# One more stick head, and the last sparse head, turned by DMA planes instead of TensorE; a gate block's halves moved up

## The chip, the cores and the metric

One core of one Trainium2 chip. The metric is device microseconds of the program, a median of three runs. In the profile the engines are PE (TensorE), ACT (ScalarE), DVE (VectorE), POOL (GpSimd) and SP (SyncE, which here only issues DMAs).

## What is computed

One block of a streaming encoder, for 512 frames of 1024 channels in f32. An input projection feeds two mixers of eight heads each:

```python
# A, sparse: the best n_sel keys of each query by an indexer's score, then softmax
logits = einsum(q, kg) * HEAD_DIM ** -0.5 + rel_bias[t5_bucket(sel - t)]
y_a = softmax(where(valid, logits, -inf)) @ vg
# B, stick-breaking: strictly causal, no softmax
log_keep = where(causal, log_sigmoid(-z), 0.0)
later = cumsum(log_keep, reverse=True) - log_keep
y_s = where(causal, exp(log_sigmoid(z) + later), 0.0) @ v
# merge, norm, gated MLP with a causal convolution of width 3, norm
merged = sigmoid(g_a + b0) * (y_a @ w_branch_dsa) + sigmoid(g_b + b1) * (y_s @ w_branch_sb)
x = layer_norm(ALPHA * x + merged @ w_out)
x = layer_norm(ALPHA * x + (gelu(causal_dwconv(x @ w_u)) * (x @ w_g)) @ w_ffn_out)
```

## The kernel before

Every f32 product goes over PE as three products of halves: a weight tile is split into a high half `whi`, rounded to PE's fast f32 format, and a rest `wlo`, and PE multiplies high by high, high by low and low by high. `Stream` (L52) loads the weight pieces in one fixed order, three ahead, into `raw`; its `_advance` (L88) has ACT write the high half (L104) and then either DVE or POOL subtract it (L113), or, for the keys in DMA_LO, ACT write minus the high half (L107) and a POOL DMA add the weights to it on landing (L110). gb0 to gb7, qa0 and ka0 go by DMA; ks1 and the four pieces of va have POOL's subtraction; qa1, ka1 and later have DVE's. `asp` says how many pieces ahead of their use are split.

The projections (`proj_t`, L227; 24 products of 128x512 each, one PSUM bank) are fillers: the list FILL orders them, and `fill` hands some of their products to PE between the steps of the heads. Stick heads 0 to 7 come first, then sparse heads a0 to a7. `tile` names in the profile drop numbers: `gb_ps` are the gate blocks of mixer B, `qa_ps` and `ka_ps` the queries and keys of the sparse heads, `va_ps` their values, which take four banks at once (`va_ps0` to `va_ps3`, the third and fourth being those that qa1 and ka1 had, free when DVE has made `qa1b` and `ka1b`). The program fixes each engine's order when it is built; `tc.issue_after(x)` keeps an instruction behind x in that order. Each engine then works strictly in its order, and an instruction that waits holds up all behind it.

A stick head h has its products z (`sb_head`, L523) turned by ACT into `keep` and `beta` (six sigmoids), scans of `keep` on DVE (`sb_sticks`, L541), and `beta` multiplied by them on POOL (L550). A sparse head has logits `l_ps` with bias and row minimum `mn` on DVE (L579), exponents on ACT (L582), and a division on DVE (L589). The weights must then be turned, so that keys lie on partitions. That goes in one of two ways:

- `turn_weights` (L439): ten transposes of 128x128 on PE into `tr_ps` (L450), three ACT copies `pth` (L453), three DVE rests `ptl` (L454). Stick heads 0 to 3 (`TURN = 4`) and a7.
- `send_planes` (L464): the f32 numbers as two planes of 16 bits. ACT copies the high ones (L469, into `keep` of the head, or `bm`), POOL or DVE the low ones (L470), and SP issues two DMA transposes into `pl` (L472). `join_planes` (L477): ACT and POOL or DVE put them together in `back` (L481, L482), ACT makes `pth` (L484), DVE `ptl` (L488). Stick heads 4 to 7, a0 to a6.

`weigh` (L498) multiplies them with the values on PE (`av_ps`, L504), eight products for a head that PE turned, ten for one that came by planes; `avt` and `yst` add the two halves up, and for every second head `ys1h`, `ys1l` split the pair.

At the first head by planes (i == TURN) ties hold the order: gb6's halves stand on ACT behind that head's `pth` (`st.behind`), ka0's copies and gb4's sigmoids behind gb6's halves. `beta`, `keep`, `bm`, `lg` and `pl`, `back`, `pth`, `ptl` have one or two buffers each, so that a head's planes wait until the head before has been read.

## Time and profile before

| | |
|---|---|
| runs (three) | median 748.91 us, 748.35 to 749.09 |
| profiled execution | 748.38 us, span 746.3 us, mean granted PE clock 0.997 |
| PE busy | 99% of the span |
| DVE, ACT, POOL busy | 76%, 54%, 20% |

A row of a timeline has the start, how long it took, engine, line, operation, out<-in by the program's names, shape, and in brackets the idle time before it and what ended that. Products on PE overlap: a row of 0.39 us is followed 0.23 us later by the next. A row of the chain has start, length and what ran.

### The profile page before, as it was taken

The numbers are of one execution on the slowest core, as the hardware profiler recorded it, in microseconds if no ns is written. First come the engines' busy times: TensorE is split into PE (matmuls) and PEld (weight loads), VectorE is DVE, ScalarE is ACT, GpSimd is POOL, SyncE is SP. The second block draws the span as 40 slices with busy tenths as digits, with TensorE's granted clock in tenths as the row PEclk, the third lists the DMA queues.
The fourth block names the chain that finished last, engine by engine and source line by source line (L and its number), as shares of the span: only waits on it lengthen the run. The fifth ranks groups of instructions, "written<-read, shape, count | busy, mean of one in ns | idle before, by whom it ended". The sixth has DMA issues, their size and how long they took to land.

```text
span 746.3 us, 9766 instructions
## 1 busy us (share of the span) xinstructions
PE 736.9 (99%) x3485; PEld 618.2 (83%) x3485; DVE 570.8 (76%) x907; ACT 406.7 (54%) x572; POOL 147.9 (20%) x161
## 2 busy tenths in 40 slices
PE   9999999999999999999999999999999999999995
PEld 7888888888888888888889888888888888888885
DVE  5569888999679898568755867676667677668995
ACT  6465867797785688645564533443444344345430
POOL 0002224365743331000101111011101101110011
PEclk9999999999999999999999999999999999999998
DMA  8445887896566554228732544444443444448532
GB/s 265 157 131 188 197 179 175 161 214 163 115 176 163 134 141 121 86 86 269 266 57 86 171 139 142 146 136 141 139 169 115 141 156 147 143 141 282 188 129 84
DMA packets 71007, 116.38 MB, mean 156 GB/s; under 512 B 39912, under 2 KB 40168, under 8 KB 70960
## 3 DMA queue, kind: packets, MB, share of 16 engines
q1 hardware_dynamic: 63680, 93.33, 41.5%
q0 software_dynamic: 5744, 18.38, 9.9%
q10 hardware_dynamic: 1536, 4.06, 2.1%
q8 instruction: 27, 0.44, 0.3%
q14 instruction: 20, 0.16, 0.1%
HBM read 95.93 MB, written 9.98 MB: 142 GB/s over the span
## 4 chain that ended last, share of the span: by engine, by line
PE 89%; DVE 4%; issue 2%; ACT 2%; POOL 2%; DMA 1%; DVEq 0%; POOLq 0%; ACTq 0%
PE u_ps L927 5%; PE u_ps L925 5%; PE g_ps L927 5%; PE g_ps L925 5%; PE u_ps L926 5%; PE g_ps L926 5%; PE m L1006 2%; PE m L1007 2%; PE m L1005 2%; PE av_ps L504 2%; PE ga_ps L235 2%; PE ga_ps L234 2%; PE gb_ps L235 2%; PE gb_ps L234 2%; PE ga_ps L233 2%
## 5 line engine op out<-in xcount | busy, mean ns | idle before, releaser
L104 ACT ACTIVATE whi<-raw 128x1024 fp32r<-128x1024 f32 (+1 forms) x124 | 124.0, 1002 | 150.3 <-PE g_ps L926 46.0
L113 DVE TENSOR_TENSOR wlo<-raw,whi 128x1024 fp32r<-128x1024 f32 (+1 forms) x105 | 123.9, 1181 | 38.7 <-ACT whi L104 38.0
L927 PE MATMUL u_ps<-x1h,wlo 128*128 128x512 f32 (+1 forms) x192 | 71.4, 372 | 0.0
L925 PE MATMUL u_ps<-x1h,whi 128*128 128x512 f32 (+1 forms) x192 | 71.3, 372 | 0.0
L926 PE MATMUL u_ps<-x1l,whi 128*128 128x512 f32 (+1 forms) x192 | 71.3, 371 | 0.0
L925 PE MATMUL g_ps<-x1h,whi 128*128 128x512 f32 (+1 forms) x184 | 69.9, 380 | 0.0
L926 PE MATMUL g_ps<-x1l,whi 128*128 128x512 f32 (+1 forms) x184 | 69.9, 380 | 0.0
L927 PE MATMUL g_ps<-x1h,wlo 128*128 128x512 f32 (+1 forms) x184 | 69.9, 380 | 0.0
L926 PEld LDWEIGHTS u_ps<-x1l,whi 128*128 128x128 f32 x192 | 36.2, 188 | 6.3
L927 PEld LDWEIGHTS u_ps<-x1h,wlo 128*128 128x128 f32 x192 | 36.2, 188 | 6.3
L925 PEld LDWEIGHTS u_ps<-x1h,whi 128*128 128x128 f32 x192 | 36.2, 188 | 6.2
L927 PEld LDWEIGHTS g_ps<-x1h,wlo 128*128 128x128 f32 x184 | 34.6, 188 | 6.6
L926 PEld LDWEIGHTS g_ps<-x1l,whi 128*128 128x128 f32 x184 | 34.6, 188 | 6.6
L925 PEld LDWEIGHTS g_ps<-x1h,whi 128*128 128x128 f32 x184 | 34.6, 188 | 6.5
L948 DVE TENSOR_TENSOR t<-raw 128x512 f32<-128x512 f32 x11 | 7.6, 692 | 38.7 <-DMA raw<-in_w_fo_dram 38.4
L562 POOL TENSOR_TENSOR bm<-win,score 128x256 f32<-128x256 f32 (+2 forms) x24 | 26.2, 1119 | 33.9 <-DMA pl<-bm 29.1
L981 DVE TENSOR_TENSOR hF<-g_ps,c 128x512 f32<-128x512 f32 x22 | 15.1, 687 | 20.9 <-PE g_ps L927 20.9
L967 POOL MEMSET u<- 128x2 f32 x22 | 2.1, 98 | 146.0 <-ACT whi L104 101.0
L973 ACT ACTIVATE c<-c,cwt 128x512 f32<-128x512 f32 x22 | 15.9, 725 | 25.2 <-DVE c L972 24.9
L823 POOL TENSOR_TENSOR rstd<-rstd,mhalf 128x1 f32<-128x1 f32 x8 | 7.7, 959 | 104.5 <-DVE rstd L822 104.5
L423 DVE MAX8 m<-score 128x8 f32<-128x256 f32 (+2 forms) x48 | 26.6, 556 | 0.9
L550 POOL TENSOR_TENSOR beta<-beta,keep 128x1280 f32<-128x1280 f32 x8 | 21.7, 2709 | 26.9 <-DVE keep L547 20.9
(578 smaller groups left out, 2086.7 us busy)
## 6 DMA issues: line engine op xcount, KB each, us to landing
raw<-in_w_fi_dram SPq DMA_DIRECT2D x44, 512.0 KB, 3.3
raw<-in_w_t_dram SPq DMA_DIRECT2D x32, 512.0 KB, 3.4
raw<-in_w_fo_dram SPq DMA_DIRECT2D x26, 512.0 KB, 4.1
wlo<-in_w_t_dram POOLq DMA_DIRECT2D x14, 512.0 KB, 5.9
raw<-in_w_br_dram SPq DMA_DIRECT2D x8, 512.0 KB, 3.7
raw<-in_w_o_dram SPq DMA_DIRECT2D x8, 512.0 KB, 4.0
raw<-in_w_v_dram SPq DMA_DIRECT2D x7, 512.0 KB, 4.5
raw_b<-in_w_fo_dram SPq DMA_DIRECT2D x6, 512.0 KB, 5.2
```

Of the source, the lines that this page charges most:

```text
L104: self.high = nc.scalar.activation(hi[:, :w], t[:, :w], AF.Copy).ins
L113: self.done[key] = eng.tensor_sub(lo[:, :w], t[:, :w], r32(hi[:, :w])).ins
L234: nc.tensor.matmul(ps[:M], wh[:, c], xl[k], start=False, stop=False)
L235: nc.tensor.matmul(ps[:M], wl[:, c], xh[k], start=False, stop=(k == KC - 1))
L423: nc.vector.max(m8, sc)
L550: nc.gpsimd.tensor_mul(beta, beta, keep[:, 1:ATT + 1])
L562: nc.gpsimd.tensor_add(bm[:, OFF[j]:OFF[j] + N], win[:, 512 - N:512], score[j])
L925: nc.tensor.matmul(ps[:, c], wh[:, kc], x1h[:, k, c], start=(k == 0), stop=False)
L926: nc.tensor.matmul(ps[:, c], wh[:, kc], x1l[:, k, c], start=False, stop=False)
L927: nc.tensor.matmul(ps[:, c], wl[:, kc], x1h[:, k, c], start=False, stop=(k == KC - 1))
L973: nc.scalar.activation(c, c, AF.Gelu_apprx_tanh, bias=cwt[:, f, 3:4])
L981: nc.vector.tensor_mul(F[:, o:o + 2].rearrange("p a b -> p (a b)"), gps_, c)
```

## The change

Stick head 3 no longer goes over PE (TURN 4 to 3), nor does a7. TIED = 4 keeps the ties of the first head by planes at head 4, and adds some. Head 3's planes are joined ahead of head 4's being sent; gb6's halves stand behind head 6's sigmoids and ahead of head 5's plane copy and head 4's `pth` (which is now made inside ka0, `finish_join`); gb4's and gb5's sigmoids stand behind the halves of gb6 and gb7; a7's planes get a buffer of their own among the `keep` tiles, and its `pth` stands behind the half that follows ga3's copies. The core of the diff:

```diff
-TURN = 4
+TURN = 3
+TIED = 4
...
-                if key == "gb6":
+                if key in ("gb6", "gb7"):
                     self.behind = self.high
...
+    def finish_join():
+        with tc.issue_after(st.highs["gb6"]):
+            parts = waiting.pop()()
+        waiting.append(parts)
+        with tc.issue_after(firsts[1]):
+            select_some(ROUNDS[TIED] - 2)
...
-    def send_planes(lg, bm, eng=nc.vector):
+    def send_planes(lg, bm, eng=nc.vector, last=False):
...
+        if last:
+            pl = padded(bp, [128, ATT + 1], tag="keep", bufs=2, name="pl")[:, 0:ATT].bitcast(U16)
+            pl = pl.rearrange("p (a b c) -> p a b c", a=2, c=128)
...
-        eng.tensor_copy(halves16(back)[:, 0], got[:, 0])
+        copied.append(eng.tensor_copy(halves16(back)[:, 0], got[:, 0]).ins)
+        if first:
+            waiting.append(lambda: halves_of(back))
+            return waiting
+        return halves_of(back)
+
+    def halves_of(back):
         th, tl = turned()
         high = nc.scalar.activation(th, back, AF.Copy).ins
...
-            return (send_planes(lg, bm) if h < H - 1 else lg), last.ins
+            return send_planes(lg, bm, last=h == H - 1), last.ins
...
+            if t == "ka0":
+                st.asp = 2
             ps = yield from proj_t(t)
...
+                if t == "ka0":
+                    st.asp = 3
+                    finish_join()
+                    st.behind = firsts[0]
+                with tc.issue_after(firsts[0]) if t == "ka0" else nullcontext():
                     qk[t] = stack_hl(ps, "k", 4, t)
...
-                with tc.issue_after(st.highs["gb6"]) if n == 4 else nullcontext():
+                with tc.issue_after(st.highs[f"gb{n+2}"]) if n in (4, 5) else nullcontext():
...
-        last = sb_sticks(*following, behind={TURN + 1: "gb5", TURN + 2: "gb6"}.get(i))
+        last = sb_sticks(*following, {TIED + 1: "gb5", TIED + 2: "gb6"}.get(i))
         if i < TURN:
             return following[0], last
+        if i == TIED + 1:
+            return following, last
...
+        if i == TIED + 1:
+            st.asp, st.behind = 3, ups[h + 1]
+            st._advance(st.used)
+            with tc.issue_after(st.highs["gb6"]):
+                weights = send_planes(*weights[0], nc.gpsimd), weights[1]
...
-        turns = w == "s" and i < TURN or not following
+        if not following:
+            fill_until("ga3")
+            with tc.issue_after(ups["ga3"]):
+                parts = join_planes(weights[0])
+            st.behind = tops[-1]
+        turns = w == "s" and i < TURN
...
+            ahead = not turns and i < TIED
+            if ahead:
+                last = sb_scans(*following)
+                with ExitStack() as ties:
+                    for ins in (last, ups[h + 1], st.high, st.added):
+                        ties.enter_context(tc.issue_after(ins))
+                    parts = join_planes(weights[0], nc.gpsimd)
+                beta, keep = following
+                with tc.issue_after(copied[-1]):
+                    nc.gpsimd.tensor_mul(beta, beta, keep[:, 1:ATT + 1])
+                with tc.issue_after(highs_of[-1]):
+                    following = send_planes(beta, keep, nc.gpsimd), last
+                joins[h + 2] = highs_of[-1]
```

The change also moves what stands on the engines. On ACT before, around the halves of gate block 6 (`whi_30`, `wlo_30`; `keep_1525` is head 5's plane copy, `pth_1582` head 4's high part, `whi_31` belongs to gb7):

```order
L348 DMA qa0b_1617<-qa0b_1617 64x1024
L469 ACTIVATE keep_1525<-beta_1524 128x1280
L484 ACTIVATE pth_1582<-back_1579 128x1280
L104 ACTIVATE whi_30_1624<-raw_30_1622 128x1024
L107 ACTIVATE wlo_30_1625<-whi_30_1624 128x1024
L338 ACTIVATE ka0a_1676<-ka0_ps_1629 64x512
L339 ACTIVATE ka0b_1677<-ka0_ps_1629 64x512
L104 ACTIVATE whi_31_1684<-raw_31_1682 128x1024
L631 ACTIVATE gb4_1755<-gb4_ps_1689,bgt_105 128x512
L107 ACTIVATE wlo_31_1685<-whi_31_1684 128x1024
```

and now (`keep_1500` is head 5's copy, `pth_1659` head 4's high part, `back_1711` joins head 5's high plane, `whi_32` is qa1's high half):

```order
L349 DMA qa0b_1595<-qa0b_1595 64x1024
L105 ACTIVATE whi_30_1637<-raw_30_1600 128x1024
L108 ACTIVATE wlo_30_1638<-whi_30_1637 128x1024
L487 ACTIVATE keep_1500<-beta_1499 128x1280
L663 ACTIVATE gb4_1748<-gb4_ps_1682,bgt_105 128x512
L508 ACTIVATE pth_1659<-back_1567 128x1280
L339 ACTIVATE ka0a_1669<-ka0_ps_1602 64x512
L340 ACTIVATE ka0b_1670<-ka0_ps_1602 64x512
L105 ACTIVATE whi_31_1677<-raw_31_1675 128x1024
L108 ACTIVATE wlo_31_1678<-whi_31_1677 128x1024
L499 ACTIVATE back_1711<-pl_1642 128x1280
L105 ACTIVATE whi_32_1752<-raw_32_1750 128x1024
```

gb6's halves went from behind head 5's copy and head 4's `pth` to ahead of both; gb4's sigmoids too come ahead of `pth`, and qa1's high half follows `back` directly, without head 7's sigmoids between.

On PE before, where gate block 7 ends and qa1 begins (`whi_32`, `wlo_32` are qa1's halves):

```order
L233 MATMUL gb7_ps_1896<-xh7_346,whi_31_1684 128x512
L234 MATMUL gb7_ps_1896<-xl7_347,whi_31_1684 128x512
L235 MATMUL gb7_ps_1896<-xh7_346,wlo_31_1685 128x512
L233 MATMUL qa1_ps_1930<-xh0_131,whi_32_1759 128x512
L504 MATMUL av_ps_1808<-pth_1721,vs0_704 128x384
L234 MATMUL qa1_ps_1930<-xl0_132,whi_32_1759 128x512
L235 MATMUL qa1_ps_1930<-xh0_131,wlo_32_1760 128x512
L573 MATMUL l_ps_1945<-ka0a_1676,qa0a_1616 128x512 x2
```

and now, where gb7 begins:

```order
L525 MATMUL av_ps_1687<-ptl_1660,vs3_713 128x128
L234 MATMUL gb7_ps_1889<-xh0_131,whi_31_1677 128x512
L235 MATMUL gb7_ps_1889<-xl0_132,whi_31_1677 128x512
L234 MATMUL qa1_ps_1923<-xh0_131,whi_32_1752 128x512
L235 MATMUL qa1_ps_1923<-xl0_132,whi_32_1752 128x512
L236 MATMUL qa1_ps_1923<-xh0_131,wlo_32_1753 128x512
L234 MATMUL qa1_ps_1923<-xh1_185,whi_32_1752 128x512
L235 MATMUL qa1_ps_1923<-xl1_186,whi_32_1752 128x512
```

qa1 went from behind all of gb6 and gb7 to behind the first two products of each; 22 of its 24 products stand there, and the rest of gb6 and gb7 follows them.

On PE before, where va takes its fourth bank (`whi_34`, `whi_35` are halves of va's first two pieces, `l_ps_2081` the last logits of a1):

```order
L270 MATMUL va_ps0_2092<-whi_35_1926,xh2_227 128x512
L270 MATMUL va_ps1_2093<-whi_35_1926,xh2_227 128x512
L270 MATMUL va_ps2_2094<-whi_35_1926,xh2_227 128x512
L270 MATMUL va_ps3_2095<-whi_34_1892,xh0_131 128x512
L271 MATMUL va_ps3_2095<-wlo_34_1893,xh0_131 128x512
L272 MATMUL va_ps3_2095<-whi_34_1892,xl0_132 128x512
L270 MATMUL va_ps3_2095<-whi_34_1892,xh1_185 128x512
L271 MATMUL va_ps3_2095<-wlo_34_1893,xh1_185 128x512
L272 MATMUL va_ps3_2095<-whi_34_1892,xl1_186 128x512
L270 MATMUL va_ps3_2095<-whi_35_1926,xh2_227 128x512
L573 MATMUL l_ps_2081<-ka0b_1677,qa0b_1617 128x256 x2
L271 MATMUL va_ps0_2092<-wlo_35_1927,xh2_227 128x512
```

and now (`va_ps3_2088` is the fourth bank, `l_ps_2074` the last logits of a1):

```order
L525 MATMUL av_ps_1973<-ptl_1833,vs3_713 128x128
L271 MATMUL va_ps2_2087<-whi_34_1885,xh0_131 128x512
L271 MATMUL va_ps3_2088<-whi_34_1885,xh0_131 128x512
L599 MATMUL l_ps_2074<-ka0b_1670,qa0b_1595 128x256 x2
L272 MATMUL va_ps0_2085<-wlo_34_1886,xh0_131 128x512
L273 MATMUL va_ps0_2085<-whi_34_1885,xl0_132 128x512
L272 MATMUL va_ps1_2086<-wlo_34_1886,xh0_131 128x512
L273 MATMUL va_ps1_2086<-whi_34_1885,xl0_132 128x512
```

Of va's products, 21 stood ahead of the fourth bank's first one and 28 ahead of a1's last logits; now three and four do, and the others follow.

More of the change, by code (lines that the diff above doesn't have):

```diff
@@ L432, in select_some @@
             pass
+    firsts, copied, highs_of, joins = [], [], [], {}
+    waiting = []
+    def finish_join():
[4 more added lines that the diff above has]
+            select_some(ROUNDS[TIED] - 2)
+    sent, tops = [], []
     def turned():
@@ L462, in halves16 @@
         return t.bitcast(U16).rearrange("p (c two) -> p two c", two=2)
-    def send_planes(lg, bm, eng=nc.vector):
+    def send_planes(lg, bm, eng=nc.vector, last=False):
         src = halves16(lg)
         own = bm[:, 0:ATT].bitcast(U16).rearrange("p (a c) -> p a c", a=2)
-        pl = bp.tile([128, 2, ATT // 128, 128], U16, tag="pl", bufs=1, name="pl")
-        nc.scalar.activation(own[:, 1], src[:, 1], AF.Copy)
+        if last:
+            pl = padded(bp, [128, ATT + 1], tag="keep", bufs=2, name="pl")[:, 0:ATT].bitcast(U16)
+            pl = pl.rearrange("p (a b c) -> p a b c", a=2, c=128)
+        else:
+            pl = bp.tile([128, 2, ATT // 128, 128], U16, tag="pl", bufs=1, name="pl")
+        sent.append(nc.scalar.activation(own[:, 1], src[:, 1], AF.Copy).ins)
+        highs_of.append(sent[-1])
         eng.tensor_copy(own[:, 0], src[:, 0])
@@ L473, in send_planes @@
         return pl
-    firsts = []
     def join_planes(pl, eng=nc.vector, first=False):
@@ L481, in join_planes @@
         nc.scalar.activation(halves16(back)[:, 1], got[:, 1], AF.Copy)
-        eng.tensor_copy(halves16(back)[:, 0], got[:, 0])
+        copied.append(eng.tensor_copy(halves16(back)[:, 0], got[:, 0]).ins)
[4 more added lines that the diff above has]
+    def halves_of(back):
         th, tl = turned()
         high = nc.scalar.activation(th, back, AF.Copy).ins
-        if first:
-            st.behind = high
-            firsts.append(high)
-        low = nc.vector.tensor_sub(tl, back, r32(th)).ins
-        if first:
-            firsts.append(low)
+        tops.append(high)
+        highs_of.append(high)
+        firsts[:] = high, nc.vector.tensor_sub(tl, back, r32(th)).ins
         h, l = (t.rearrange("p (s c) -> p s c", c=128) for t in (th, tl))
@@ L536, in sb_head, with sb_scans @@
             c = slice(OFF[grp[0]], OFF[grp[0]] + o)
-            nc.scalar.activation(keep[:, c], ps[:, :o], AF.Sigmoid, scale=-0.125)
+            with tc.issue_after(joins[h]) if h in joins else nullcontext():
+                nc.scalar.activation(keep[:, c], ps[:, :o], AF.Sigmoid, scale=-0.125)
             ups[h] = nc.scalar.activation(beta[:, c], ps[:, :o], AF.Sigmoid, scale=0.125).ins
         return beta, keep
-    def sb_sticks(beta, keep, behind=None):
+    def sb_scans(beta, keep):
         for j in (1, 0, 2, 3):
@@ L548, in sb_sticks @@
                                                 op1=ALU.max)
+        return scan.ins
+    def sb_sticks(beta, keep, behind=None):
+        last = sb_scans(beta, keep)
         with tc.issue_after(st.done[behind]) if behind else nullcontext():
             nc.gpsimd.tensor_mul(beta, beta, keep[:, 1:ATT + 1])
-        return scan.ins
+        return last
     def dsa_head(q, k, h):
@@ L625, in filler @@
             elif kind in ("ks", "ka"):
-                with tc.issue_after(st.highs["gb6"]) if t == "ka0" and firsts else nullcontext():
+                if t == "ka0":
[3 more added lines that the diff above has]
+                with tc.issue_after(firsts[0]) if t == "ka0" else nullcontext():
                     qk[t] = stack_hl(ps, "k", 4, t)
@@ L701, in values_of @@
         fill_until(f"v{w}")
-        ends = weigh(parts, vals[w], h, pair[w])
+        ends = weigh(parts.pop() if parts is waiting else parts, vals[w], h, pair[w])
         if h % 2 == 1:
@@ L725, in tile_block @@
             ends = values_of(*joined)
-        turns = w == "s" and i < TURN or not following
+        if not following:
[4 more added lines that the diff above has]
+        turns = w == "s" and i < TURN
         if turns:
-            if not following:
-                fill(GAP)
             parts, lows = turn_weights(weights[0])
         if w == "s" and i + 1 < H:
-            with tc.issue_after(lows) if turns else nullcontext():
-                following = advance(i + 1)
+            ahead = not turns and i < TIED
[11 more added lines that the diff above has]
+                joins[h + 2] = highs_of[-1]
+            else:
+                with tc.issue_after(lows) if turns else nullcontext():
+                    following = advance(i + 1)
             with tc.issue_after(following[1]):
-                if not turns:
+                if not turns and not ahead:
                     with tc.issue_after(ups[h + 1]), tc.issue_after(st.high):
-                        parts = join_planes(weights[0], nc.gpsimd, i == TURN)
-                if i == TURN:
+                        parts = join_planes(weights[0], nc.gpsimd, i == TIED)
+                if i == TIED:
                     select_some(2)
-                    with tc.issue_after(firsts[1]):
-                        select_some(ROUNDS[i] - 2)
                 else:
@@ L751, in tile_block @@
                     with ExitStack() as ties:
-                        for ins in (emptied["va"] if (w, h) == ("a", 1) else ()) + (following[1], ups[(h + 1) % H]):
+                        late = (emptied["va"] if (w, h) == ("a", 1) else ()) + ((sent[-1],) if i + 2 == len(heads) else ())
+                        for ins in late + (following[1], ups[(h + 1) % H]):
                             ties.enter_context(tc.issue_after(ins))
```

4 lines of the change are left out of this document (2 added, 2 removed).

## The prediction

> **What bounds the kernel now.** I read the page first, then the waits of the tensor engine (PE), then the chain of waits in the stretch that the change rewrites, then timelines of single engines. The page gives busy time, and the chain that ended last by engine:
>
> ```profile
> PE 736.9 (99%) x3485; PEld 618.2 (83%) x3485; DVE 570.8 (76%) x907; ACT 406.7 (54%) x572; POOL 147.9 (20%) x161
> ```
>
> ```profile
> PE 89%; DVE 4%; issue 2%; ACT 2%; POOL 2%; DMA 1%; DVEq 0%; POOLq 0%; ACTq 0%
> ```
>
> All that PE waited for, in the view of waits (us in total, times, longest):
>
> ```profile
> PE idle_ps L210 <- DVE idle L207: 1.2, 1, 1.2
> PE bs_ps L603 <- DVE ka2b L341: 0.4, 1, 0.4
> PE bs_ps L605 <- DVE wlo L113: 0.2, 1, 0.2
> ```
>
> PE is the bound: work taken from it is time, unless a new wait gives it back. But in one stretch the others are nearly as late as PE. The chain of waits leaves PE with the first two of these rows and comes back with the last two:
>
> ```profile
> 189.74 1.25 POOL ys2l L517
> 190.99 3.61 POOL wlo L113
> ```
>
> ```profile
> 253.70 0.70 DVE ka2b L341
> 254.54 0.47 PE bs_ps L603
> ```
>
> Between 190 and 254 us a chain over GpSimd (POOL), ScalarE (ACT), VectorE (DVE) and transposes runs as long as PE's own work there; PE has under a microsecond to spare. Whoever moves that chain against PE's order pays, and the change moves both.
>
> **The change part by part.** *PE's pace.* The 24 products of ka1 begin between the first two of these rows of PE (the third is used further down):
>
> ```profile
> 186.68 0.39 PE L233 MATMUL ka_ps<-xh,whi 128*128 128x512 f32 x1
> ```
>
> ```profile
> 192.12 0.39 PE L270 MATMUL va_ps<-whi,xh 128*128 128x512 f32 x1
> ```
>
> ```profile
> 200.94 0.41 PE L573 MATMUL l_ps<-ka0b,qa0b 128*128 128x256 f32 x2
> ```
>
> (192.12 − 186.68) / 24 = 0.227 us for 512 columns.
>
> *Transposes off PE, head 3 and a7.* A head's ten transposes in the tile's view, and PE's rows around head 3:
>
> ```profile
> L450 PE MATMUL tr_ps<-ident,lg x10: 272/272/273, 308.5 to 309.5; 128*128 128x128 f32 x10
> ```
>
> ```profile
> 133.60 1.25 PE L450 MATMUL tr_ps<-ident,beta 128*128 128x128 f32 x10
> 134.61 0.47 PE L234 MATMUL gb_ps<-xl,whi 128*128 128x512 f32 x1
> ```
>
> By starts they take 134.61 − 133.60 = 1.01 us, and the product behind them lasts 0.08 longer than the usual 0.39: 1.1 us a head. Against that, weights times values goes as ten products in place of eight, over the same 2 x 1280 columns, 1.14 us at the pace. A head with ten took, in the chain,
>
> ```profile
> 256.75 1.33 PE av_ps L504 x10
> ```
>
> so the two extra cost between 0 and 0.2 us; I take 0.1, since eight already pay part of the surplus. Net −1.0 us for head 3 and −1.0 for a7, on the binding engine.
>
> A rule of the Trainium skill speaks against this: VectorE: DVE Perf Modes, section The three transpose paths, gives 390 ns for a 128x128 transpose on TensorE and 1309 ns by DMA, and the page's rules for kernel authors prefer TensorE where the result may land in PSUM. By its figures ten would be 3.9 us of PE and each head would save 2.8 us more, and the slower DMA would matter only where PE waits for it. The row differs: the ten follow each other at 0.10 us. The sum goes by the row.
>
> *Cover of the two new round trips.* PE's gb3 ended, and the copy behind which head 3's high part now stands began, at
>
> ```profile
> 139.27 0.39 PE L233 MATMUL qa_ps<-xh,whi 128*128 128x512 f32 x1
> ```
>
> ```profile
> 140.78 1.05 ACT L107 ACTIVATE wlo<-whi 128x1024 fp32r<-128x1024 f32 x1
> ```
>
> so the part is there at 140.78 + 1.05 + 1.26 = 143.1, while PE does 36 products of qa0 and ka0 first: 139.27 + 36 x 0.227 = 147.4. Four microseconds of cover; if the transposes took that much longer, their excess would be paid. For a7 the high part stands on ACT behind a half that waits for gate block ga4; between that and a7's products PE does ga5, 24 x 0.227 = 5.4 us, against 1.04 + 1.26 + 1.5 for half, high and low part. Both cost 0; 0.7 is the most that I would give a7, were its transposes late.
>
> *The first products of qa1.* PE's new order puts 22 products of qa1 ahead of most of gate block 6. They need both halves of raw_32. ACT makes the high one behind head 5's `back` copy, which waits for head 5's planes, whose copy now stands behind gb6's halves. ACT's rows, before:
>
> ```profile
> 150.76 1.68 ACT L481 ACTIVATE back<-pl 128x1280 uint16<-128x1280 uint16 x1 [0.99 <-DMA pl<-keep]
> ```
>
> ```profile
> 156.20 1.27 ACT L469 ACTIVATE keep<-beta 128x1280 uint16<-128x1280 uint16 x1 [0.18 <-POOL keep L470]
> 157.38 1.26 ACT L484 ACTIVATE pth<-back 128x1280 fp32r<-128x1280 f32 x1
> 158.54 1.04 ACT L104 ACTIVATE whi<-raw 128x1024 fp32r<-128x1024 f32 x1
> ```
>
> ```profile
> 164.41 1.65 ACT L481 ACTIVATE back<-pl 128x1280 uint16<-128x1280 uint16 x1
> ```
>
> From `back` to the copy of head 5 (`keep`) took 156.20 − 150.76 = 5.4 us. Now avt and ys1h of the second pair (estimated 1.2 together) and gb6's two halves (2.1) stand in between: the copy begins at 150.76 + 5.4 + 3.3 = 159.5 and ends at 160.7. From pth to the next `back` took 164.41 − 157.38 = 7.0, now without gb6's halves 4.9: ACT is free at 165.6. The transposes of the copy land 4.9 behind it, also at 165.6 (issues by queue, 120 to 200 us):
>
> ```profile
> pl<-keep SPq DMA_TRANSPOSE x8, 4.9
> ```
>
> `back` (1.6 with its overlap), the high half (1.04) and DVE's low half,
>
> ```profile
> 173.88 1.21 DVE L113 TENSOR_TENSOR wlo<-raw,whi 128x1024 fp32r<-128x1024 f32 x1
> ```
>
> end at 169.5. PE comes to its first product with that low half at 168.0, from gb5's last three products, which began at
>
> ```profile
> 166.93 0.40 PE L233 MATMUL gb_ps<-xh,whi 128*128 128x512 f32 x1
> ```
>
> 166.93 − 1.0 + (3 + 6) x 0.227: the six are two each of gb6, gb7 and qa1. So PE would wait 1.5 us. But head 4's planes, which set 150.76, went with both transposes back to back; a load now parts them, and the first may land a microsecond sooner, which leaves 0.5. I take the middle, s = 1.0, with the ends 0 and 3 (every landing a microsecond later).
>
> *The wait for ka1's bank.* PE's new order has, behind qa1 and ka1, one product for each of va's four banks and then the last logits of sparse head a1; before, 28 products of va stood ahead of the logits. The fourth bank is ka1's, free when DVE has made ka1b, and the logits wait for the row minimum right behind ka1b on DVE. Without a wait PE would come to the logits 24 products earlier than 200.94: 200.94 − 1.0 − 24 x 0.227 + s = 194.5 + s. When is the minimum there? ACT and DVE before:
>
> ```profile
> 183.13 1.28 ACT L582 ACT_TABLE_LOAD   x1
> ```
>
> ```profile
> 184.94 0.59 ACT L509 ACTIVATE avt<-av_ps 64x512 f32<-64x512 f32 x1
> ```
>
> ```profile
> 186.48 0.63 ACT L516 ACTIVATE ys2h<-yst 128x512 fp32r<-128x512 f32 x1 [0.95 <-DVE yst L510]
> ```
>
> ```profile
> 188.45 1.26 ACT L484 ACTIVATE pth<-back 128x1280 fp32r<-128x1280 f32 x1
> ```
>
> ```profile
> 189.74 2.60 DVE L488 TENSOR_TENSOR ptl<-back,pth 128x1280 fp32r<-128x1280 f32 x1
> ```
>
> ```profile
> 197.51 0.69 DVE L341 TENSOR_TENSOR ka1b<-ka_ps,ka1b 64x512 fp32r<-64x512 f32 x1
> 198.23 0.69 DVE L579 CUSTOM_DVE_ANT_0 lg<-l_ps,bm 128x512 f32<-128x512 f32 x1
> ```
>
> In the new order ACT's high half for va waits for gate block 7's products, which now end behind qa1's 22: with ka1, two of qa1 and 2560 columns of logits still to come before va, at 192.12 − 1.0 − (24 + 2 + 5) x 0.227 = 184.1 + s. Behind it ACT has that half and gb7's sigmoids (1.6), table load and exponent (184.94 − 183.13 = 1.8), then ys2h, a half and qa1a (188.45 − 186.48 = 2.0): pth runs from 189.5 to 190.7 and DVE's ptl begins there. In the row it took 2.60, beside POOL's wlo of 190.99. Alone, the one and the other took
>
> ```profile
> 204.58 1.49 DVE L488 TENSOR_TENSOR ptl<-back,pth 128x1280 fp32r<-128x1280 f32 x1 [1.04 <-ACT pth L484]
> ```
>
> ```profile
> 181.46 2.40 POOL L113 TENSOR_TENSOR wlo<-raw,whi 128x1024 fp32r<-128x1024 f32 x1 [3.95 <-ACT whi L104]
> ```
>
> Now POOL's wlo begins about 189 and is out by 191.5 if nothing holds it. The Trainium skill, SBUF — State Buffer, section Who interferes with whom, has a DVE instruction with two inputs in SBUF and a GpSimd one that reads SBUF shut each other out for a whole instruction; by that ptl would begin at 191.5 and end at 193.0. By the rows it ends between 192.2 and 193.3; I take 192.6. From its end to ka1b's end it was 198.20 − 192.34 = 5.9 us, of which one exponent, 0.6, now stands earlier: 5.3, and 0.75 for the minimum. So 198.6 + s, and PE waits 198.6 − 194.5 = 4.1 us whatever s is; ends 3.7 and 4.8. Everything on PE is queued behind it: 92 products of va, whose halves are out by 188.
>
> *What comes back.* PE, late by 4 us, no longer meets its old waits at 227 and 254:
>
> ```profile
> 226.48 0.39 PE L604 MATMUL bs_ps<-ys0l,whi 128*128 128x512 f32 x1
> 227.06 0.50 PE L605 MATMUL bs_ps<-ys0h,wlo 128*128 128x512 f32 x1 [0.19 <-DVE wlo L113]
> ```
>
> There 0.58 − 0.23 = 0.35, and 0.5 at 254 (the wait of 0.4 and its restart): −0.9, or nothing if the chain slips as far as PE.
>
> *Sum:* −1.0 (head 3) + 1.0 (s) + 4.1 − 0.9 − 1.0 (a7) = +2.2 us. The profiled execution took 748.38 us (span 746.3), 0.53 below the median of the runs, 748.91; 748.91 + 2.2 = 751.1. The ends: −1.0 + 0 + 3.7 − 0.9 − 1.0 = +0.8 and −1.0 + 3.0 + 4.8 − 0.9 − 1.0 = +4.9: 749.7 to 753.8.
>
> **The rivals.** *The saving is kept* (ends faster). The minimum is there when PE comes, 4 us sooner than I sum, so ka1's bank holds nothing up. For it: PE's 99%, products removed are time. Against it: ACT's steps from gb7 to ka1b fill 10 to 12 us without a gap. It decides once the wait is under 1.0 us; with none it gives −2.0 to −2.9, 746.0 to 746.9. Chance 0.16.
>
> *Hidden by the chain.* No such wait, but the chain of 190 to 254 still ends at 254.5, so that head 3's microsecond is waited away and a7's alone is kept: −1.0, 747.9. For it the chain of waits, against it the same bank. Chance 0.10.
>
> *The clock falls in the wait.* At the start, after idling, nine products of 512 columns lasted
>
> ```profile
> 1.19 4.01 PE L210 MATMUL idle_ps<-idle 128*128 128x512 bf16 x9 [1.19 <-DVE idle L207]
> ```
>
> 4.0 / 9 = 0.44 us each, twice the pace. If the same follows the wait, 4 us at half pace cost 2.0 more: +4.2, 753.1. No row has PE idle so long in mid-run. The Trainium skill, TensorE: Matmul & The Clock Gate, Part 1, has the clock halve after one idle window of about 3.4 us; a wait of 4.1, broken by one product, is at that edge. Chance 0.14.
>
> **How the numbers follow.** The forecast has 0.60. About 0.2%, 1.5 us, is what a measurement of this kernel can tell from no change. Of the forecast's own range, 749.7 to 753.8, seven tenths lie over +1.5: 0.42, and the falling clock's 0.14 make slower 0.56. Same: 0.18 + 0.10. Faster: 0.16. The range, 746.8 to 753.8, leaves out most of the first rival and the far end of the third.
>
> **What would show it.** Right: in PE's waits a row of 3 to 5 us in all for va_ps and l_ps behind DVE ka1b and its minimum, a smaller one for qa_ps, none for bs_ps and av_ps; 30 products left of tr_ps with beta, none with lg. If PE waits under 1 us near 195, the main term is wrong; if its products last twice as long behind the wait, the third rival holds.

## The result and the profile after

The changed kernel took 760.01 us (median of four runs, 759.52 to 760.56) against 749.00 for the kernel before on the same chip: a ratio of 1.0145, interval 1.0133 to 1.0157. It is 11.0 us slower where 2.2 were forecast, outside the range. The profiled execution took 760.56 us, 12.2 more than the profiled one of before.

The page, busy time and the chain that ended last:

```profile
PE 740.2 (98%) x3469; PEld 619.1 (82%) x3469; DVE 573.7 (76%) x905; ACT 410.9 (54%) x572; POOL 149.2 (20%) x163
...
PE 87%; DVE 7%; ACT 2%; issue 2%; DMA 2%; ACTq 0%; SPq 0%; DVEq 0%
```

PE has 16 instructions fewer and is busy 3.3 us longer: something made its products slower. What PE waited for:

```profile
PE va_ps L271 <- DVE ka1b L342: 3.6, 1, 3.6
PE qa_ps L234 <- ACT whi L105: 3.2, 1, 3.2
PE av_ps L525 <- DVE ptl L511: 1.4, 1, 1.4
...
PE vs_ps L271 <- ACT whi L105: 1.0, 1, 1.0
PE av_ps L525 <- ACT pth L508: 0.6, 1, 0.6
```

The two waits of before for `bs_ps` are gone, as forecast; the row for `va_ps` behind `ka1b` is the forecast one, and `qa_ps` waits too, but three times as long. New are the two `av_ps` rows, which the prediction's signs excluded: they are head 6's weights (the seventh group of `av_ps`; head 7's comes at 219 us, though the expected texts of e3 and e17 below call these head 7's). The `vs_ps` row lies at 6 us, far from the change; in the runs below it is 0.7 or less. PE's timeline around the two long waits:

```profile
168.49 0.40 PE L235 MATMUL gb_ps<-xl,whi 128*128 128x512 f32 x1
172.10 0.80 PE L234 MATMUL qa_ps<-xh,whi 128*128 128x512 f32 x1 [3.21 <-ACT whi L105]
172.69 0.63 PE L235 MATMUL qa_ps<-xl,whi 128*128 128x512 f32 x1
...
197.62 0.61 PE L271 MATMUL va_ps<-whi,xh 128*128 128x512 f32 x2
...
201.77 0.44 PE L525 MATMUL av_ps<-ptl,vs 128*128 128x384 f32 x1 [1.42 <-DVE ptl L511]
...
203.03 0.45 PE L271 MATMUL va_ps<-whi,xh 128*128 128x512 f32 x1
207.09 0.77 PE L271 MATMUL va_ps<-whi,xh 128*128 128x512 f32 x1 [3.62 <-DVE ka1b L342]
207.73 0.79 PE L599 MATMUL l_ps<-ka0b,qa0b 128*128 128x256 f32 x2
208.32 0.63 PE L272 MATMUL va_ps<-wlo,xh 128*128 128x512 f32 x1
208.75 0.63 PE L273 MATMUL va_ps<-whi,xl 128*128 128x512 f32 x1
...
213.01 0.39 PE L271 MATMUL va_ps<-whi,xh 128*128 128x512 f32 x1
```

Behind both waits products start 0.43 us and more apart, where 0.23 is the usual pace. Windows of the same stretches (the column behind POOL's is the granted clock; all four were 1.00 before):

```profile
168.00:172.00 4.00, 0.89 (x6) 0.45 (x4) 3.10 (x7) 2.49 (x2) 0.88 (x1) 1.00 1.23 219
172.00:176.00 4.00, 3.87 (x9) 2.66 (x10) 2.52 (x5) 2.07 (x5) 0.70 (x1) 0.57 1.11 267
203.00:207.00 4.00, 0.48 (x4) 0.16 (x2) 1.40 (x3) 3.08 (x5) 2.62 (x2) 0.89 0.30 66
207.00:213.00 6.00, 5.91 (x14) 4.51 (x15) 5.08 (x12) 3.44 (x6) 2.69 (x4) 0.50 0.00 0
```

The clock was halved from 172.0 to 175.4 and from 206.2 to 213.0; the second price is half of 213.01 − 207.09, 3.0 us, the first 1.7. By starts of products, the waits cost 3.4 at qa1, 0.8 and 1.6 at head 6's weights and 3.8 at the bank: 9.6 in all. With 4.7 for the clock, and −1.0, −0.9 and −1.6 for head 3, the old waits and a7 (measured below, where the old wait at 254 us is gone too, so that up to 0.5 is counted twice), that is +10.8 against the 11.0 measured.

ScalarE after, from head 4's `back` to the half for which PE waited at 172, and head 6's `pth`:

```profile
150.33 1.67 ACT L499 ACTIVATE back<-pl 128x1280 uint16<-128x1280 uint16 x1
155.24 0.60 ACT L357 ACTIVATE qa0b<-qa_ps 64x512 fp32r<-64x512 f32 x1 [3.24 <-DVE qa0a L358]
...
161.56 1.25 ACT L487 ACTIVATE keep<-beta 128x1280 uint16<-128x1280 uint16 x1
...
169.51 1.63 ACT L499 ACTIVATE back<-pl 128x1280 uint16<-128x1280 uint16 x1 [1.70 <-DMA pl<-keep]
171.01 1.03 ACT L105 ACTIVATE whi<-raw 128x1024 fp32r<-128x1024 f32 x1
...
197.56 1.26 ACT L508 ACTIVATE pth<-back 128x1280 fp32r<-128x1280 f32 x1
```

and VectorE after, from head 6's scans (x4, from the start of the first to the end of the last) to `ka1b`:

```profile
157.43 5.57 DVE L569 TENSOR_TENSOR_SCAN keep<-keep,first 128x512 f32<-128x512 f32 x4
164.59 2.31 DVE L511 TENSOR_TENSOR ptl<-back,pth 128x1280 fp32r<-128x1280 f32 x1 [1.59 <-ACT pth L508]
...
175.28 0.06 DVE L547 MEMSET keep<- 128x1 f32 x1 [1.38 <-issue]
...
192.59 0.43 DVE L427 TENSOR_SCALAR score<-score 128x512 f32<-128x512 f32 x1
193.05 0.69 DVE L531 TENSOR_TENSOR yst<-av_ps,avt 64x512 f32<-64x512 f32 x1
...
198.84 2.87 DVE L511 TENSOR_TENSOR ptl<-back,pth 128x1280 fp32r<-128x1280 f32 x1
...
206.25 0.69 DVE L342 TENSOR_TENSOR ka1b<-ka_ps,ka1b 64x512 fp32r<-64x512 f32 x1
```

Head 4's `back` is as early as before (150.33, 150.76). From there on everything is late: head 5's copy by 5.4 us, its `back` by 5.1, the last step of the selection (`score`) by 8.3 (184.32 before), `ka1b` by 8.7 (197.51).

### The profile page after: what moved, and what is told of

Read it like the earlier page. It is cut to its first block, busy times and chain, and to the rows that moved or that the text cites. A ratio compares the mean times of both kernels' runs of the same rounds, so it can differ in the third digit from the quotient of the medians.

```text
span 758.7 us, 9748 instructions
## 1 busy us (share of the span) xinstructions
PE 740.2 (98%) x3469; PEld 619.1 (82%) x3469; DVE 573.7 (76%) x905; ACT 410.9 (54%) x572; POOL 149.2 (20%) x163
## 4 chain that ended last, share of the span: by engine, by line
PE 87%; DVE 7%; ACT 2%; issue 2%; DMA 2%; ACTq 0%; SPq 0%; DVEq 0%
PE u_ps L982 5%; PE u_ps L980 5%; PE g_ps L982 5%; PE g_ps L980 5%; PE u_ps L981 5%; PE g_ps L981 5%; PE m L1061 2%; PE m L1062 2%; PE m L1060 2%; PE ga_ps L236 2%; PE ga_ps L235 2%; PE ga_ps L234 2%; PE o_ps L910 2%; PE o_ps L909 2%; PE o_ps L911 2%
## 5 line engine op out<-in xcount | busy, mean ns | idle before, releaser
L569 DVE TENSOR_TENSOR_SCAN keep<-keep,first 128x512 f32<-128x512 f32 (+3 forms) x32 | 28.0, 922 | 0.1
```

Of the source, the lines that this page charges most:

```text
L569: scan = nc.vector.tensor_tensor_scan(rev, rev, first[:, 512 - N:512][:, ::-1], 0.0, op0=ALU.mult, op1=ALU.max)
```

## The experiments

Two questions: what costs the time on PE (its new order, or the halved clock), and why the other engines' chain is late (the moved halves of gb6, VectorE's load, or head 3's trip through the planes). Except where a source edit says otherwise, each kernel is the changed one, with every engine's order held to the changed kernel's but for the rows shown. Differences "against the changed kernel" are from its 760.01. The kernel before took 748.87 to 749.09 beside them.

### PE's order: qa1's products, va's products, both

Edit of e1, on PE: qa1's 22 products behind the 22 of gate block 6 that followed them (first and last rows).

```diff
 L235 MATMUL gb_ps<-xl_132,whi_1677 128x512
+L236 MATMUL gb_ps<-xh_131,wlo_1638 128x512
...
+L236 MATMUL gb_ps<-xh_346,wlo_1638 128x512
 L234 MATMUL qa_ps<-xh_131,whi_1752 128x512
```

> The changed kernel, every engine in its order, but on PE the 22 products of qa1 and the 22 of gb6 behind them change places. Theory A (PE's order): the waits at 169 and 198 to 207 us are two faults of PE's order and add up; the first goes, with the half clock behind it: 3.4 + 1.9 = 5.3 less, 754.7. Theory B (a late chain): DVE's rounds of key selection, which end at 193, set when pth, ptl and ka1b are there; PE comes 5.3 us sooner to va and waits as much longer there: 760.0, within 0.7.

Measured 758.33 us, ratio 1.0118 (1.0101 to 1.0135): −1.7. The wait at qa1 is gone with its half clock, and PE came to va 4.5 us sooner (193.16), but `ka1b` only 3.1 (203.19). The difference came back as waits (2.3 for the bank, 2.1 and 0.4 for head 6's weights, 1.3 for head 5's), with the clock halved for 13.7 us.

Edit of e2, on PE: 24 products of va's other banks ahead of the fourth bank's first and of a1's last logits, much as before.

```diff
 L271 MATMUL va_ps_2087<-whi_1885,xh_131 128x512
-L271 MATMUL va_ps_2088<-whi_1885,xh_131 128x512
-L599 MATMUL l_ps<-ka0b,qa0b 128x256 x2
 L272 MATMUL va_ps_2085<-wlo_1886,xh_131 128x512
...
 L273 MATMUL va_ps_2087<-whi_1919,xl_228 128x512
+L271 MATMUL va_ps_2088<-whi_1885,xh_131 128x512
+L599 MATMUL l_ps<-ka0b,qa0b 128x256 x2
```

> The changed kernel, every engine in its order, but on PE 24 products of va in its first three banks stand ahead of the fourth bank's first product and of a1's last logits. The wait of 3.8 us for ka1's bank is covered by 24 x 0.227 = 5.4 us of work and the clock does not fall behind it (3.0): 6.8 less, 753.2. The same by theory A and theory B; under B some of it may come back at a0's weights, up to 2 us.

Measured 753.82, ratio 1.0065 (1.005 to 1.008): −6.2. The waits that are left:

```profile
PE qa_ps L234 <- ACT whi L105: 2.5, 1, 2.5
...
PE av_ps L525 <- DVE ptl L511: 0.9, 2, 0.7
PE av_ps L525 <- ACT pth L508: 0.7, 1, 0.7
```

The bank's row is gone and the clock behind it stays whole. So the forecast's main term is real, and with its clock it is worth 6.2 us, not 4.1.

The edit of e3 is e1's, and goes further than e2's: of va's other banks 22 products now stand ahead of and among head 6's weights, and more behind them, all ahead of the fourth bank.

```diff
 L271 MATMUL va_ps_2086<-whi_1885,xh_131 128x512
+L272 MATMUL va_ps_2085<-wlo_1886,xh_131 128x512
...
+L271 MATMUL va_ps_2086<-whi_1919,xh_227 128x512
 L525 MATMUL av_ps<-pth,vs_704 128x384
...
+L273 MATMUL va_ps_2086<-whi_1919,xl_252 128x512
 L525 MATMUL av_ps<-ptl,vs_704 128x384
```

> Both moves on PE, and va's products laid so that each stands where its halves are there (12 of the first piece and 2 of the second ahead of head 7's weights, 10 more ahead of their low part). Theory A: all of the waits and both falls of the clock go, 9.6 + 4.8 less: 745.6. Theory B: PE comes to va at 192.8 and waits for va's first low half until 196.8, where POOL stands behind the selection; 4.0 of wait and 1.6 of half clock stay, and about 1 behind it: 752, within 2.

Three runs took 752.29, 753.58 and 756.65 (a fourth, of 1501.52, is left out); ratio 1.0069 (1.0042 to 1.0097). PE now waits 3.3 us for head 7's `pth` (at 207) and 1.3 for head 5's `ptl` (at 183). With PE's order repaired at both places the kernel is still 3 to 8 us slower than before.

### The clock: useless products in the wait

28 products of zeros by zeros, 256 columns each, added into va's third bank between its first product and the fourth bank's.

```diff
+                if which == "va" and (k, i) == (0, 2):
+                    for _ in range(28):
+                        nc.tensor.matmul(pss[i][:, :256], zero[:, :128], zero, start=False, stop=False)
```

> The changed kernel, all in their order, with 28 products of zeros by zeros (256 columns each, some 3.2 us) added into va's third bank in PE's wait for ka1's bank. If the clock falls because PE idles, it stays whole behind the wait: 3.0 less, 757.0. If it falls for another reason, or the added work delays PE: 760 or more.

Measured 755.94, ratio 1.0093 (1.0076 to 1.011): −4.1 for adding work. Its windows:

```profile
172.00:176.00 4.00, 3.96 (x11) 3.18 (x12) 3.95 (x8) 3.88 (x9) 3.78 (x2) 0.61 0.78 220
203.00:207.00 4.00, 3.29 (x16) 2.35 (x15) 3.85 (x11) 1.20 (x4) 3.48 (x5) 1.00 0.02 4
207.00:213.00 6.00, 6.00 (x28) 4.97 (x27) 4.91 (x11) 3.99 (x5) 1.99 (x1) 1.00 0.57 95
```

The clock is whole where the changed kernel had 0.50, and still halved behind qa1's wait, which was left alone. So the halved clock is a price of the wait, 3.0 us by the rows at the bank. The other microsecond is not explained: in the profiled execution `ka1b` came 3.2 us sooner (203.01) and head 6's weights in time, both ahead of anything that the zeros could hasten.

### gb6's halves back, and rounds of the selection early

Edit of e5, on ScalarE (on SP, head 5's first transposes go up one load with it): gb6's halves behind head 5's copy and head 4's `pth`, as before.

```diff
+L487 ACTIVATE keep<-beta 128x1280
+L508 ACTIVATE pth<-back 128x1280
 L105 ACTIVATE whi_1637<-raw_1600 128x1024
 L108 ACTIVATE wlo_1638<-whi_1637 128x1024
-L487 ACTIVATE keep<-beta 128x1280
 L663 ACTIVATE gb_1748<-gb_ps,bgt 128x512
-L508 ACTIVATE pth<-back 128x1280
```

> The changed kernel with PE, DVE and POOL in their order; on ACT gate block 6's halves stand again behind head 5's plane copy and head 4's high part, and SP issues that copy's two transposes one behind the other, ahead of the next loads. Theory C1 (the moved halves made the chain late): the copy and the high part come 2 to 2.7 us sooner, the wait at qa1 falls from 3.4 to about 1 with no half clock behind it (4.3 less), and ka1b comes as much sooner, so the wait for it stays: 755 to 756. Theory C2 (DVE's own order and the longer transposes make it late): 760, within 1.

Measured 760.99, ratio 1.0168 (1.0147 to 1.0188): nothing gained. The wait at qa1 fell to 1.6 and 0.5 and the halved clock behind it went, but PE waits 1.5 for head 5's `ptl`, 2.0 and 0.9 for head 6's weights and 2.3 for the bank, with the clock halved for 13.7 us. Head 5's second transposes still stand behind va's first load, other than the expected text has it; e6 below moves them. The moved halves, or the transposes that went with them here, have a share in the wait at qa1; moving them back alone wins nothing.

Edit of e4, on VectorE: three rounds of the selection into the gaps at 164.6, 172.1 and 175.3 (shown is one).

```diff
-L511 TENSOR_TENSOR ptl<-back,pth 128x1280
 L424 MAX m_1663<-score_370 128x8
+L425 MATCH_REPLACE score_370<-m_1663,score_370 128x512
+L511 TENSOR_TENSOR ptl<-back,pth 128x1280
```

> The changed kernel, PE, ACT, POOL and SP in their order; on DVE three rounds of the key selection are moved up into the gaps at 163, 171 and 174 us, where DVE waits. Theory A: PE's order is what waits, so 760.0, within 1. Theory B: the selection ends 4.2 us sooner, and with it ys2, pth, ptl and ka1b; PE's wait of 3.8 falls under the length that brings the clock down: 4.2 + 3.0 less, 753 to 756.

Measured 759.86 (758.59 to 763.84), ratio 1.0154 (1.0126 to 1.0183). In the profiled execution (758.59, the fastest) the waits for head 6's weights fell from 2.0 to 0.2 and PE came out of the bank's wait 2 us sooner, at 205.3, but that wait stayed as long (3.6); the median shows nothing of it. The rounds have a share in the weights' waits; for the rest this run decides nothing.

### Each half of the change alone

Edit of e7, from the kernel before: only a7 by planes (core of it).

```diff
-            return (send_planes(lg, bm) if h < H - 1 else lg), last.ins
+            return send_planes(lg, bm, last=h == H - 1), last.ins
...
-        turns = w == "s" and i < TURN or not following
+        if not following:
+            fill_until("ga3")
+            with tc.issue_after(ups["ga3"]):
+                parts = join_planes(weights[0])
+            st.behind = tops[-1]
+        turns = w == "s" and i < TURN
```

> The kernel before, with a7 alone by planes (head 3 over PE, gate block 6's halves in their old place). If PE is the bound there and the planes are there in time: 1.0 less than before, 748.0. If the products' two more pieces or a wait eat it: 749.0. If a7's weights come late: up to 2 more, 751.

Measured 747.29 (746.6 to 747.95), ratio 0.9979 (0.997 to 0.9988): −1.6, or −0.9 to −2.2, faster than both kernels. All that PE waits for, apart from the start, is

```profile
PE bs_ps L612 <- DVE wlo L113: 0.2, 1, 0.2
```

so a7's round trip is covered, as forecast.

Edit of e8, from the kernel before: only head 3 by planes, with the old ties at head 4 and none of the new.

```diff
-TURN = 4
+TURN = 3
+TIED = 4
...
-                        parts = join_planes(weights[0], nc.gpsimd, i == TURN)
-                if i == TURN:
+                        parts = join_planes(weights[0], nc.gpsimd, i == TIED)
+                if i == TIED:
```

> The kernel before with TURN 3 and nothing else: head 3 by planes, a7 over PE, gate block 6's halves and all ties as before, and each engine's order as the program finds it. If the ties and the moved halves made the change slow (C1): near 748, head 3's own 1.0 less. If a round trip more on ACT, POOL and DVE between 140 and 195 us makes the chain late whatever the ties (C2): 753 to 760, with waits of PE at va again.

Measured 759.67, ratio 1.0143 (1.0129 to 1.0157). Its orders differ from the changed kernel's, its waits lie elsewhere, and it costs the same:

```profile
PE gb_ps L236 <- DMA wlo<-in_w_t_dram: 3.7, 2, 2.4
PE av_ps L505 <- DVE ptl L489: 2.5, 1, 2.5
PE av_ps L505 <- ACT pth L485: 2.2, 1, 2.2
```

The 2.5 are for head 3's own weights, which the changed kernel covers. ScalarE shows a reason for the others: the second transposes of head 4 were issued at 147.44 and landed 16.2 us later, and behind them ScalarE stood still:

```profile
163.76 0.60 ACT L538 ACTIVATE keep<-z_ps 128x512 f32<-128x512 f32 x1 [9.63 <-DMA pl<-keep]
```

So a7 alone loses nothing, and head 3 alone loses as much under the old ties as the whole change under the new, though not by the same waits. The new ties with head 3 still over PE were not run.

### One late link at a time

Edit of e6, on SP: both transposes of head 5 ahead of va's first load. e9 does the same for head 4's pair as well (shown).

```diff
-L491 DMA_TRANSPOSE pl<-keep 128x10x128
+L491 DMA_TRANSPOSE pl<-keep 128x10x128 x2
 L74 DMA raw_1750<-in_w_t_dram 128x1024
-L491 DMA_TRANSPOSE pl<-keep 128x10x128
 L74 DMA raw_1850<-in_w_t_dram 128x1024
-L491 DMA_TRANSPOSE pl<-keep 128x10x128
+L491 DMA_TRANSPOSE pl<-keep 128x10x128 x2
 L74 DMA raw_1883<-in_w_v_dram 128x1024
-L491 DMA_TRANSPOSE pl<-keep 128x10x128
```

> The changed kernel, all in their order, but SP issues both transposes of head 5's planes ahead of va's first load, which parts them in the changed kernel. If the parting is what made them late, the second lands about 4 us sooner (175.2 there), DVE's gap of 1.4 at 174 closes and the chain comes 1.4 to 3 sooner: 757 to 758.6. If the transposes are late because the loads share the queues, the first lands later and nothing is won: 760, within 1.

Measured 757.51, ratio 1.012 (1.0107 to 1.0134): −2.5, within the first expectation; the wait at qa1 fell to 2.4.

> The changed kernel, all in their order, but SP issues both transposes of head 4's planes one behind the other, and both of head 5's; in the changed kernel a weight load stands between each pair. Theory C3 (the load between them makes head 4's second plane 4.6 us late, and every later link inherits it): head 4's second plane lands near 152, pth and ptl, the selection and ka1b come 4 us sooner or more, the wait at qa1 falls under 1: 752 to 755. If only head 5's pair counted: as in the run with that pair alone, 757.5. If the load's delay costs as much as the pairs win: 760.

Measured 757.76, ratio 1.0118 (1.0103 to 1.0133): −2.3, no more than head 5's pair alone. Head 4's second plane landed at 151.5, not 156.4, and ScalarE still waited 3.4 us for VectorE's `qa0a`.

Edit of e13, on VectorE: qa0's two subtractions, for which ScalarE waited 3.24 us, ahead of scans and rounds. e14 is this and e9's edit together.

```diff
 L569 SCALAR_TENSOR_TENSOR keep<-keep,first 128x512
+L358 SCALAR_TENSOR_TENSOR qa0a<-qa_ps,qa0a 64x512
...
 L425 MATCH_REPLACE score_370<-m_1570,score_370 128x512
+L358 SCALAR_TENSOR_TENSOR qa0b<-qa_ps,qa0b 64x512
...
-L358 SCALAR_TENSOR_TENSOR qa0a<-qa_ps,qa0a 64x512
 L425 MATCH_REPLACE score_370<-m_1573,score_370 128x512
-L358 SCALAR_TENSOR_TENSOR qa0b<-qa_ps,qa0b 64x512
```

> The changed kernel, all in their order, but on DVE the two subtractions of qa0 stand three and two places of head 5's scans further up, so that ACT does not wait 3.2 us (152 to 155.2) for them. Theory C4 (two links are late by the same: these subtractions, and head 4's second plane, which frees the buffer of head 6's sigmoids at 156.4): the sigmoids start at 156.4 all the same, 759 to 760. Theory C5 (the subtractions alone hold ACT): 3.2 less, 756.5 to 757.

Measured 758.43 (755.96 to 758.9), ratio 1.0121 (1.0102 to 1.0139): between the two expectations, undecided.

> The same, and both pairs of transposes together on SP (757.8 by themselves). Theory C4: with both links gone, head 6's sigmoids, gate block 6's halves, head 5's copy and head 4's high part come 3 us sooner than with the pairs alone; the wait at qa1 goes with its half clock, that for ka1's bank stays: 753.5 to 755. Theory C5: as much sooner as by the subtractions alone. If another link is as late: 757.8.

Measured 757.73, ratio 1.0119 (1.0104 to 1.0134). ScalarE's chain did come sooner (the half for qa1 at 167.9, not 171.0), and PE then waited for the other half, on VectorE:

```profile
PE qa_ps L236 <- DVE wlo L114: 3.0, 1, 3.0
```

That low half took 2.77 us beside GpSimd's work, 1.23 in the changed kernel. Undoing one link uncovers the next, about as late.

### The repairs together

Four combinations of the edits shown: e9, e2 and e4; e9 and e3; e9, e13 and e2; e9, e13 and e3.

> The changed kernel with three repairs at once: both pairs of transposes together on SP, 24 products of va ahead of its fourth bank and a1's last logits on PE, three rounds of the key selection moved up on DVE. Theory C3 with the wait for ka1's bank covered: no half clock left, a wait of a microsecond or two at qa1 and at head 7's weights: 748 to 750, head 3's trip paid back but nothing won against a7 alone, 747.3. If head 3's trip can be hidden whole: 746.3. If the chain stays late: 752 to 754.

Measured 754.10, ratio 1.0066 (1.0051 to 1.0081).

> The changed kernel with both pairs of transposes together on SP, qa1 behind gate block 6 and va's products laid as in the run with both moves on PE, which gave 752 to 757. If the chain now comes 4 us sooner, its waits at head 6's and head 7's weights (1.4 and 3.4) go: 747 to 749. If the chain is as late as there: 752 to 754.

Measured 753.12, ratio 1.0053 (1.0038 to 1.0068); PE waits 3.3 for head 7's `pth`, in one piece, and the clock falls behind it.

> The same, and 24 products of va ahead of its fourth bank and a1's last logits, which took 6.2 off the changed kernel. Theory C4: 747 to 749, with under 2 us of PE's waits left between 160 and 215 us. If the chain is still late: 752 to 754.

Measured 753.46, ratio 1.0064 (1.0047 to 1.0081).

> The same two moves on SP and DVE with qa1 behind gate block 6 and va's products laid as in the run with both moves on PE (753.1 with the pairs). Theory C4: head 7's weights, for which PE waited 3.4 there, come 3 us sooner: 748 to 750. If the chain is still late: 752 to 754.

Measured 753.34 (751.67 to 755.16), ratio 1.006 (1.0039 to 1.008); what PE waits for is now a third link, gate block 6's low half by DMA:

```profile
PE gb_ps L236 <- DMA wlo<-in_w_t_dram: 2.5, 1, 2.5
```

All four missed what was expected if these links were all that is late, and lie at the 752 to 754 of a chain that is still late. No version with head 3 by planes came nearer than 4 us to the kernel before, by its median.

### VectorE's load

The last five of the sixteen rounds of the last block of the selection on 32 columns, in the changed kernel (e17) and in the kernel before (e18, order not held).

```diff
-        for _ in range(NSEL // 8):
+        for r in range(NSEL // 8):
...
-            nc.vector.max(m8, sc)
-            nc.vector.match_replace(sc, m8, sc, TAKEN)
+            part = sc[:, 0:32] if j == 3 and r >= 11 else sc
+            nc.vector.max(m8, part)
+            nc.vector.match_replace(part, m8, part, TAKEN)
```

> The changed kernel, every engine's order held, with the last five of the sixteen rounds of the last block of key selection done on 32 columns in place of 512: part of the selection is left out, some 5 to 6.5 us of VectorE's work between 182 and 193 us, which stands ahead of head 7's sums and weights and of ka1b. Theory 'VectorE's load': what makes head 7's weights and ka1b late is that VectorE, full from 130 us on, comes to them late; then PE's waits at va (2.4 and 3.8 us) and the half clock behind them (3.0) go almost whole, the wait at qa1 (3.4) and its half clock (1.9) stay: 751 to 754 us. Rival 'chain': they are late by way of ScalarE, GpSimd and the transposes, and VectorE would only wait in their place: 757 to 760 us, with ka1b no more than 2 us sooner than 206.9.

Measured 757.12, ratio 1.0103 (1.0086 to 1.012): −2.9, short of the first theory and at the edge of the second. Its wait for the bank and VectorE's rows:

```profile
PE va_ps L271 <- DVE ka1b L342: 3.6, 1, 3.6
```

```profile
189.96 0.70 DVE L532 TENSOR_TENSOR yst<-av_ps,avt 64x512 f32<-64x512 f32 x1 [0.98 <-ACT avt L531]
...
203.37 0.69 DVE L342 TENSOR_TENSOR ka1b<-ka_ps,ka1b 64x512 fp32r<-64x512 f32 x1
```

VectorE was through with the rounds four microseconds sooner, waited for ScalarE, and `ka1b` came 2.9 sooner, more than the 2 that the rival allowed; head 6's weights came in time, the bank did not. So these five rounds account for at most 2.9 of `ka1b`'s 8.7 us; how the rest divides this run does not show. The bank's row could hardly shrink: from the end of head 6's `ptl` to the end of `ka1b` it is 5.2 us here as in the changed kernel, and PE, which reaches those weights just as `ptl` ends, has some 1.7 us of products in between.

> The kernel before with the same five rounds on 32 columns (part of the selection left out): what the same work is worth where PE does not wait for VectorE. Both theories: within 0.5 us of the kernel before, 748.3 to 749.3. If it is 2 us or more faster, the gain of its fellow in this job is not one of the change's waits alone.

Measured 751.04, ratio 1.0024 (1.0014 to 1.0034): 2 us slower for less work. It is no clean control: with less work VectorE's order was built anew, and the division of a1's weights (196.18, 5.16 us in four) now stands ahead of `ka1b` (202.07, before 197.51):

```profile
PE va_ps L270 <- DVE ka1b L341: 2.1, 1, 2.1
```

By chance it repeats the forecast's main term in the kernel before: the bank late by 4.6 us, a wait of 2.1, a clock halved for 3.4 us.

## Why the prediction was right on the sign and wrong on the size

*Direction, and the main wait: right, its size in part by luck.* PE waits for the fourth bank behind `ka1b`, once, in the row forecast, 3.8 us where 4.1 were worked out. The last link was read well: from the end of head 6's `ptl` (201.71) to the end of `ka1b` it was 5.2 us, 5.3 in the working. What stands ahead of it was not. By the working, with s = 1.0, gate block 7 ends at 185.1 and that head's `pth` begins at 190.5; they did at 190.58 and 197.56. The first 5.5 us are mostly PE's own: 2.4 more at qa1, 1.7 of half clock, 1.0 at 6 us. The other 1.6 are ScalarE's wait for the `yst` at 193.05, behind VectorE's selection, which was over at 185.7 before, was left out of the working, and now ends at 193.0. PE came to the bank 8 us late as well, in part because it stood for the same `ptl`, and so the difference came out. Head 6's weights, put at nothing, cost 2.4.

*"Both cost 0", the cover of the two new round trips: failed for head 3.* The step compared head 3's own products with its own weights, and there it held in the changed kernel: none of PE's waits is for head 3. It did not ask what the trip's steps on the other engines push back. ScalarE and GpSimd each get 2.9 us more to do there (a plane copy, a half of `back`, and on ScalarE one `pth` for three copies), and SP a pair of transposes. VectorE gets no more, one `ptl` of 1.47 us for three rests of 1.62 together, but at 147.77 in place of 135.76, ahead of `qa0a`, and in a stretch in which, in windows of before, it was busy all the time:

```profile
130.00:150.00 20.00, 19.49 (x40) 1.00 0.81 153
150.00:160.00 10.00, 9.81 (x21) 1.00 0.90 204
160.00:170.00 10.00, 9.76 (x17) 1.00 1.04 240
170.00:180.00 10.00, 9.93 (x15) 1.00 0.64 137
```

There was no slack there to make up for a late input. After, VectorE is less busy in the same windows, since it stands waiting for what comes late:

```profile
160.00:170.00 10.00, 8.30 (x10) 1.00 0.86 179
170.00:180.00 10.00, 7.70 (x12) 0.83 0.75 150
```

Head 5's chain, head 6's weights, the selection and `ka1b` all slid by 5 to 9 us. So where the step has nothing, the sum of the rows has 2.4 more at qa1, 2.4 at head 6's weights and 4.7 of half clock. e7 and e8 show that a kernel loses this much with head 3 by planes and nothing with a7; e5, e6, e9, e13 and e14 that no one link among those moved carries it, as several are about equally late.

*The first products of qa1, s = 1.0 with ends 0 and 3: mis-sized.* Measured 3.4 us. The copy was put at 159.5 and began at 161.56: ScalarE waited 3.24 us for `qa0a`, where the 5.4 us taken from before held 0.34 of such a wait. The transposes were taken at 4.9 us; from the copy's end at 162.8 to `back` at 169.51 it was 6.7. Both durations were taken from the profile of before.

*The clock: a rival that came true, twice.* It had 0.14, and 2.0 us; it cost 1.7 and 3.0. A forecast of a 4 us wait ought to have held it: in all these runs every stop of PE of 2.7 us or more was followed by a halved clock. The Trainium skill, TensorE: Matmul & The Clock Gate, Part 1, was named there with a window of about 3.4 us; the lengths of the halved stretches here, 3.4 and 6.8, agree with it.

*PE's savings: right as far as seen.* a7's −1.0 lies within the −0.9 to −2.2 measured, in which the old wait at 254 us has a part. Head 3's −1.0 cannot be seen by itself. The old waits went: −0.9.

*What stays open:* how the slide divides among VectorE's load (at most 2.9 of 8.7 at `ka1b` for the rounds of e17), operations that take longer beside others, and slower landings. The scans of head 6 show the second:

```profile
156.30 2.37 DVE L547 TENSOR_TENSOR_SCAN keep<-keep,first 128x512 f32<-128x512 f32 x3
...
159.23 0.68 DVE L547 TENSOR_TENSOR_SCAN keep<-keep,first 128x256 f32<-128x256 f32 x1
```

Before, with GpSimd idle, these four took 3.05 us; after, in the row shown above, 5.57, while GpSimd copied planes and split a pair. That GpSimd's work is the reason is not shown: no run took it away by itself.

## What to carry to other kernels

Work moved from the bound engine to others is free only if the others have slack where it lands: look at their busy time in that stretch, not over the span, and follow every queue that the new steps push back, not only the result's own way. A wait of two microseconds or more on TensorE is to be priced with the clock that may halve behind it; work kept for that place, or even products that do nothing, can spare the second price. When several links are about equally late, undoing one shows almost nothing; the halves of a change run alone (here a7 for, head 3 against) tell more.
